# A one-layer S5 / RG-LRU trunk on one core: w_out's first sums one block sooner, one block split by VectorE, three columns at the head of gate's first half

## The chip, the cores and the metric

One core of a Trainium2 chip runs the whole program. The metric is the device time of one execution in microseconds (us), and the figure of a kernel is the median of its runs; smaller is better. The kernel before takes 932.66 us, the median of 3 runs (932.24 to 932.68).

## What is computed

The reference is one decoder layer over 1024 tokens and 1024 channels in float32. What matters here is its end:

```python
merged = jax.nn.sigmoid(gate_s) * z_s + jax.nn.sigmoid(gate_l) * z_l
x = x + rms_norm(merged @ w_out[i], g_post[i])
x = x + (p[i] @ w_ple[i]) * jax.nn.sigmoid(x @ w_ple_gate[i])
return x
```

So two products of 1024 x 1024 matrices follow each other (w_out, then w_ple_gate), and between them stands a normalisation over the channels, whose statistic needs all channels of a token.

## The kernel before

**Arithmetic.** Channels lie on the partitions, tokens on the free axis. Every float32 factor is split into two fp32r parts, hi (ScalarE's rounding copy) and lo (the rest), and `three` (L314 to L318) issues three matmuls of 128x128 by 128x512 for a block: hi by hi (L316), then hi of the weights by lo of the data and lo of the weights by hi of the data (L318). The product with w_out (like that with w_bl) is done by a recursion that needs fewer block products: seven products of quarters instead of eight, with sums of quarters of the weights (S1 to S4) and of the data (T1 to T4).

**Weights.** `weight_plan` writes the order of all weights down as a list of *quads* of four 128x128 blocks each, which TensorE takes one after the other. A "plain" quad is half of a chunk of eight blocks. The quads "O2", "S3", "S1", "S4" or "O4" belong to a pair of chunks and hold sums of them. The class `Weights` serves the list: `fetch` loads chunks on SP's queue into four raw tiles (`wraw`, 512 KB each), and a raw tile is loaded again only when all quads made from it are split; `sum` lets GpSimd add up the sums (tensor_tensor at L194, float32, both inputs in SBUF: S1 = A21 + A22, S2 = S1 - A11, S3 = A11 - A21, S4 = A12 - S2); `make` writes the hi part on ScalarE (L222) into a ring of six tiles (`wq`); the lo part comes in one of two ways. For plain quads of `BY_DMA` (w_bs, w_out, w_ple_gate, except for the last 16 quads) ScalarE writes the negative of the source (L225) and a DMA issued by GpSimd adds the source minus hi in the memory's path (L226, `accum_op=add`):

```python
if q[0] == "plain" and BLOCKS[q[1][0]][0] in self.BY_DMA and i < len(QUADS) - 2 * ND:
    nc.scalar.activation(lo, src, AF.Copy, scale=-1.0)
    nc.gpsimd.dma_start(lo.bitcast(F32), src, accum_op=ALU.add)
else:
    self.owed.append((i, lo, src, hi))
```

For all others VectorE subtracts (`lows`, L234). `ahead`, called before each product, makes quads up to four further than TensorE's place, splits one fewer, and starts sums up to two further than that. `sum` returns at an "O2" quad when the quad before it isn't made yet (L186).

**Order of the work.** TensorE, VectorE, ScalarE and GpSimd run their instructions in the order in which the program writes them (a manual schedule); pieces of background work (`bg`, generators) are advanced by `tick` after each product. The part around the change:

1. The product with w_out. Four products into banks oX (B11; quads 0 to 3 of w_out), two more into the first two oX banks (B21; quads 4 and 5; these are the last plain quads ahead of the sums), then four groups of oY, oZ, oW and oV with the sums S2, S3, S1 and S4. Meanwhile VectorE and ScalarE finish the data's parts: `t_raw` (L1385 to L1393) forms T2 and T3 of the last row, `t1_ops` T1. `op_split` takes hi on ScalarE (L1364) and lo on VectorE (L1371).
2. Six more products into oV, while `post_half(1)` normalises the tokens of half 1: it forms x1 (L1562, L1563) and its parts hi (L1364) and lo (L1371), eight rows one after the other.
3. `gate_half(1)`: columns of w_ple_gate by x1 of half 1. Its first two columns run over the rows 0 to 3 of x1 first (columns 0, 1), then over rows 4 to 7 (columns 0, 1), so that TensorE has work while the later rows are formed; then come columns 2 to 7 one by one. Beside it `post_half(0)` squares the last six rows of half 0 (ScalarE L1484, VectorE adds them to ssq, L1489) and TensorE sums them over the channels (`pst_post`, L388), ahead of column 4. `finish` (L1588 to L1592) takes a column out: sigmoid on ScalarE, which needs another activation table (ACT_TABLE_LOAD), a product and a sum on VectorE (L1590, L1591), and the store.
4. `gate_half(0)`: the eight columns by x1 of half 0.

In the prediction, "gate's quad 0, 1, ..." counts the quads of item 3 in TensorE's order; quad 4 is the first whose lo part is made after the last row of x1.

Of the kernel before, what the change touches and what calls it, by code (L numbers as in the profile page):

```python
# [20 lines left out]
ND = 8  # L21
# [15 lines left out]
def weight_plan():  # L37
    blocks, quads = [], []

    def chunk(names):  # L40
        first = len(blocks)
        blocks.extend(names)
        return (first, len(names))

    def cut(c):
        for o in range(0, c[1], 4):
            quads.append(("plain", c, o, min(4, c[1] - o)))

    def col(name, m, ks):
        return [(name, k, m) for k in ks]  # L50

    def plain(names):
        for o in range(0, len(names), 8):
            cut(chunk(names[o:o + 8]))

    for m in range(0, ND, 2):
        plain(col("w_ple", m, range(2)) + col("w_ple", m + 1, range(2)))
    lo, hi = range(4), range(4, ND)
    plain(col("w_in", 0, lo) + col("w_in", 1, lo))
    plain(col("w_in", 2, lo) + col("w_in", 0, hi))  # L60
    plain(col("w_in", 1, hi) + col("w_in", 2, hi))
    plain(col("w_in", 3, range(ND)))
    for m in (*range(36, 44), *range(28, 36), 4, 5):
        plain(col("w_in", m, range(ND)))

    def gated(m, head):
        c = chunk(col("w_in", m, range(ND)))
        quads.append(("plain", c, 0, 4))
        if head >= 0:
            plain([("w_a", head, 0), ("w_x", head, 0)])  # L70
        quads.append(("plain", c, 4, 4))

    for m in range(NL):
        gated(8 + m, m - 1)
        plain(col("w_in", 18 + m, range(ND)))
    gated(6, NL - 1)
    plain(col("w_in", 7, range(ND)))
    hi2 = range(8, NL)
    for ks in (lo, hi2, hi):
        if ks is hi2:  # L80
            plain([b for m in range(0, ND, 2) for b in col("w_bl", m, hi2)])
            continue
        for m in (0, 4):
            plain(col("w_bl", m, ks) + col("w_bl", m + 2, ks))
    for j in range(NS):
        plain(col("w_glu", 4 + j, range(NS)) + col("w_glu", j, range(NS)))
    for m in range(0, ND, 2):
        c0, c1 = (chunk(col("w_bl", m + i, range(8))) for i in range(2))
        for part in ("O2", "S1", "P", "S3", "S4", "A22"):
            if part == "P":  # L90
                plain(col("w_bl", m, hi2) + col("w_bl", m + 1, hi2))
            else:
                quads.append((part, c0, c1, 4))
    for n in range(0, ND, 2):
        plain([b for d in F_ROWS[n:n + 2] for b in col("w_bs", d, range(NS))])

    def outs(m, ks):
        cut(chunk(col("w_out", m, ks) + col("w_out", m + 2, ks)))

    for m, ks in ((0, lo), (4, lo), (0, hi)):  # L100
        outs(m, ks)
    for m in range(0, ND, 2):
        c0, c1 = (chunk(col("w_out", m + i, range(ND))) for i in range(2))
        quads.extend((part, c0, c1, 4) for part in ("O2", "S3", "S1", "O4" if m else "S4"))
    for m, ks in ((1, hi), (5, hi), (4, hi)):
        outs(m, ks)
    cs = [chunk(col("w_ple_gate", m, range(ND))) for m in range(ND)]
    for h in range(2):
        if not h:
            for ks in (lo, hi):  # L110
                cut(chunk(col("w_ple_gate", 0, ks) + col("w_ple_gate", 1, ks)))
        for c in cs[0 if h else 2:]:
            cut(c)
    return blocks, quads

# [15 lines left out]


LAST = chunk_users()


class Weights:
# [42 lines left out]
    def sum(self, upto):  # L179
        G = self.nc.gpsimd  # L180
        while len(self.ready) <= min(upto, len(QUADS) - 1):
            i = len(self.ready)
            self.fetch(i)
            q = QUADS[i]
            s = self.sums
            if q[0] == "O2" and len(self.done) < i:  # L186
                return

            def add(name, a, b, op, into=None):
                if into is None:  # L190
                    s[name] = self.tmp.tile([P, HT], F32, tag=name, name=f"w{name}_{i}")
                else:
                    s[name] = s[into]
                G.tensor_tensor(s[name], s[a], s[b], op)  # L194

            if q[0] == "plain":
                _, c, o, n = q
                self.ready.append((self.raws[c][:, o * P:(o + n) * P], n))
                continue
            if q[0] in FIRST:  # L200
                r0, r1 = (self.raws[c] for c in q[1:3])
                s.update(A11=r0[:, :HT], A12=r0[:, HT:], A21=r1[:, :HT], A22=r1[:, HT:])
            if q[0] == "O2":
                self.lows(i)
                add("S1", "A21", "A22", ALU.add)
                add("S2", "S1", "A11", ALU.subtract)
            if q[0] in ("S4", "O4"):
                add("S4", "A12", "S2", ALU.subtract, "S2")
            if q[0] == "S3":
                add("S3", "A11", "A21", ALU.subtract, "A21")  # L210
            self.ready.append((s[q[0].replace("O", "S")], 4))

    def make(self, upto):
        nc = self.nc
        while len(self.done) <= min(upto, len(QUADS) - 1):
            i = len(self.done)
            self.sum(i)
            src, n = self.ready[i]
            t = self.ring.tile([P, 2, 4, P], F32R, tag="q", name=f"wq{i}")
            hi = t[:, 0].rearrange("p b m -> p (b m)")[:, :n * P]  # L220
            lo = t[:, 1].rearrange("p b m -> p (b m)")[:, :n * P]
            nc.scalar.activation(hi, src, AF.Copy)  # L222
            q = QUADS[i]
            if q[0] == "plain" and BLOCKS[q[1][0]][0] in self.BY_DMA and i < len(QUADS) - 2 * ND:
                nc.scalar.activation(lo, src, AF.Copy, scale=-1.0)  # L225
                nc.gpsimd.dma_start(lo.bitcast(F32), src, accum_op=ALU.add)  # L226
            else:
                self.owed.append((i, lo, src, hi))
            self.done.append(t)
# [23 lines left out]
def tile_hybrid_trunk(  # L253
# [1315 lines left out]
    def gate_half(h, hl):  # L1569
        def rhs(k, _):  # L1570
            return hl(0, k), hl(1, k)

        first = {}
        if h:
            for n in range(4):
                q, m = n // 2, n % 2
                if not q:
                    first[m] = bank(f"ps_pg{h}{m}")
                W.ahead()
                for b, wb in enumerate(W.next()):  # L1580
                    three(first[m], wb, rhs(4 * q + b, h), q + b == 0, q * b == 3)
                tick()
        for m in range(ND):
            pl = plp[:, m % 4, :]
            nc.sync.dma_start(pl, ple_d[m][:, HALF[h]])
            sb = sbp[:, m % 4, :]

            def finish(ps, cs):  # L1588
                S.activation(sb[:, cs], ps, AF.Sigmoid)
                V.tensor_tensor(sb[:, cs], sb[:, cs], pl[:, cs], ALU.mult)  # L1590
                V.tensor_tensor(sb[:, cs], sb[:, cs], x1(m, h)[:, cs], ALU.add)  # L1591
                nc.sync.dma_start(out[m * P:(m + 1) * P, h * HT + cs.start:h * HT + cs.stop], sb[:, cs])  # L1592

            if h or m < ND - 1:
                finish(first.get(m) or plain(ND, rhs, f"pg{h}{m}", (h,))[h], slice(0, HT))
                continue
            W.ahead()
            wq = [W.next(), W.next()]
            for c in range(2):
                ps = bank(f"ps_pgz{c}")[:, :HT // 2]  # L1600
                cs = slice(c * HT // 2, (c + 1) * HT // 2)
                for k in range(ND):
                    three(ps, wq[k // 4][k % 4], [v[:, cs] for v in rhs(k, h)], k == 0, k == ND - 1)
                if c == 0:
                    finish(ps, cs)
                    continue
                cut = [slice(HT // 2, HT // 2 + P), slice(HT // 2 + P, HT)]
                for i, q in enumerate(cut):
                    S.activation(sb[:, q], ps[:, i * P:(i + 1) * P], AF.Sigmoid)
                for q in cut:  # L1610
                    V.tensor_tensor(sb[:, q], sb[:, q], pl[:, q], ALU.mult)
                    V.tensor_tensor(sb[:, q], sb[:, q], x1(m, h)[:, q], ALU.add)
                nc.sync.dma_start(out[m * P:(m + 1) * P, h * HT + cs.start:h * HT + cs.stop], sb[:, cs])
# [81 lines left out]
```

## Time and profile before

| | |
|---|---|
| median of 3 runs | 932.66 us (932.24 to 932.68) |
| the profiled execution | 932.37 us |
| its span, first to last instruction | 930.6 us |
| TensorE busy | 923.1 us, 99% of the span |
| VectorE, ScalarE, GpSimd busy | 625.0, 469.6, 150.3 us |
| mean granted TensorE clock | 0.999 of full speed |
| the chain that ended last | 96% TensorE, 2% VectorE |

The span is counted from the first to the last instruction on the core; the time of the execution has some 1.8 us around it. The page gives busy time by engine, the trace gives single instructions: start, duration, engine, line, what is written and read, and in brackets how long the engine had been idle before and which instruction released it. TensorE's durations are modelled: matmuls overlap, so a step of three matmuls takes less than the sum of its rows, and the distance from one start to the next is what counts.

### The profile page before, as it was taken

The page shows a single profiled execution, that of the slowest core. Times are in us where ns is not written, and L with a number is a line of the kernel's source. Part 1 is how long each engine was busy: PE and PEld are TensorE (multiplying, and loading weights), DVE is VectorE, ACT ScalarE, POOL GpSimd, SP SyncE. Part 2 cuts the span into 40 slices and gives each one's busy share as a digit, 9 for nine tenths or more (in the row PEclk, how much of TensorE's full clock was granted, in tenths as well). Part 3 has the DMA queues.
Part 4 walks back from the last instruction along what each step waited for, and adds up shares of the span by engine and source line. Part 5 has one row for each costly group of instructions (what it writes and reads, how often), then busy time and mean ns, then how long its engine had stood idle before and what let it go on. Part 6 is the DMA issues. An engine that isn't in the chain of part 4 may idle for free.

```text
span 930.6 us, 11716 instructions
## 1 busy us (share of the span) xinstructions
PE 923.1 (99%) x4228; PEld 759.7 (82%) x4228; DVE 625.0 (67%) x977; ACT 469.6 (50%) x714; POOL 150.3 (16%) x159
## 2 busy tenths in 40 slices
PE   9999999999999999999999999999999999999997
PEld 7888888888888888888888888888888887887876
DVE  6985566666664446776666667687862798886863
ACT  6643233444443257666666668444434355558531
POOL 1318012212220000000000000022322126422100
PEclk9999999999999999999999999999999999999999
DMA  9745456554623211111111117811479965499951
GB/s 356 277 126 158 126 141 168 173 166 138 178 90 107 74 29 52 51 51 45 52 51 51 52 44 208 296 41 57 141 261 238 271 164 203 122 244 231 301 181 52
DMA packets 70442, 134.21 MB, mean 144 GB/s; under 512 B 18416, under 2 KB 32880, under 8 KB 70384
## 3 DMA queue, kind: packets, MB, share of 16 engines
q1 hardware_dynamic: 64768, 122.72, 41.5%
q0 software_dynamic: 5472, 10.49, 6.5%
q8 instruction: 33, 0.54, 0.2%
q10 hardware_dynamic: 144, 0.26, 0.1%
q14 instruction: 25, 0.20, 0.1%
HBM read 95.30 MB, written 27.53 MB: 132 GB/s over the span
## 4 chain that ended last, share of the span: by engine, by line
PE 96%; DVE 2%; issue 0%; DMA 0%; ACT 0%
PE ps_L L318 16%; PE ps_L L316 8%; PE ps_rg L318 8%; PE ps_rx L318 8%; PE ps_pg L318 6%; PE ps_rx L316 4%; PE ps_rg L316 4%; PE ps_F L318 3%; PE ps_u L318 3%; PE bZ L318 3%; PE ps_pg L316 3%; PE pg L318 2%; PE bW L318 2%; PE bX L318 2%; PE ps_ple L318 2%; PE ps_ea L318 2%
## 5 line engine op out<-in xcount | busy, mean ns | idle before, releaser
L318 PE MATMUL ps_L<-hB,wq 128*128 128x512 f32 x640 | 197.4, 390 | 0.0
L318 PEld LDWEIGHTS ps_L<-hB,wq 128*128 128x128 f32 x640 | 120.2, 188 | 24.5
L316 PE MATMUL ps_L<-hB,wq 128*128 128x512 f32 x320 | 127.0, 397 | 0.0
L222 ACT ACTIVATE wq<-wraw 128x512 fp32r<-128x512 f32 (+1 forms) x188 | 112.5, 614 | 24.3 <-issue 9.4
L234 DVE TENSOR_TENSOR wq<-wraw,wq 128x512 fp32r<-128x512 f32 (+1 forms) x152 | 104.0, 700 | 3.2 <-ACT wq L222 3.2
L318 PE MATMUL ps_rg<-hB,wq 128*128 128x512 f32 x320 | 98.7, 390 | 0.0
L318 PE MATMUL ps_rx<-hB,wq 128*128 128x512 f32 x320 | 98.7, 390 | 0.0
L318 PE MATMUL ps_pg<-x1hl,wq 128*128 128x512 f32 x240 | 75.2, 394 | 0.5 <-DVE x1hl L1371 0.5
L316 PEld LDWEIGHTS ps_L<-hB,wq 128*128 128x128 f32 x320 | 60.1, 188 | 13.4 <-issue 1.7
L318 PEld LDWEIGHTS ps_rg<-hB,wq 128*128 128x128 f32 x320 | 60.1, 188 | 12.9
L318 PEld LDWEIGHTS ps_rx<-hB,wq 128*128 128x128 f32 x320 | 60.1, 188 | 12.9
L1075 DVE SCALAR_TENSOR_TENSOR c<-ps_rx,cp_t,c 128x1023 f32<-128x1023 f32 (+2 forms) x30 | 38.5, 1282 | 47.6 <-ACT c L1073 46.9
L194 POOL TENSOR_TENSOR wS<-wraw 128x512 f32<-128x512 f32 x8 | 11.9, 1486 | 356.8 <-DMA wraw<-w_blocks 349.4
L316 PE MATMUL ps_rx<-hB,wq 128*128 128x512 f32 x160 | 62.5, 391 | 0.0
L316 PE MATMUL ps_rg<-hB,wq 128*128 128x512 f32 x160 | 62.5, 391 | 0.0
L318 PEld LDWEIGHTS ps_pg<-x1hl,wq 128*128 128x128 f32 x240 | 44.7, 188 | 11.8 <-DVE x1hl L1371 1.8
L1012 ACT ACTIVATE sg<-ps_L 128x1024 f32<-128x1024 f32 x20 | 20.5, 1026 | 59.6 <-issue 52.5
L226 POOL DMA_DIRECT2D wq<-wraw x36 | 31.8, 883 | 100.7 <-ACT wq L225 68.7
L316 PE MATMUL ps_pg<-x1hl,wq 128*128 128x512 f32 x120 | 47.1, 393 | 0.0
L318 PE MATMUL ps_u<-hB,wq 128*128 128x512 f32 x128 | 39.7, 392 | 0.4 <-DVE hB L733 0.4
L318 PE MATMUL ps_F<-ys,wq 128*128 128x512 f32 x128 | 39.4, 389 | 0.0
L1083 ACT ACT_TABLE_LOAD x9 | 11.5, 1283 | 51.2 <-DVE yr L1112 51.2
(360 smaller groups left out, 1930.4 us busy)
## 6 DMA issues: line engine op xcount, KB each, us to landing
wraw<-w_blocks SPq DMA_DIRECT2D x95, 512.0 KB
wq<-wraw POOLq DMA_DIRECT2D x36, 256.0 KB, 5.5
xt<-x_t SPq DMA_DIRECT2D x8, 512.0 KB
ple_d<-ple_sb SPq DMA_DIRECT2D x8, 512.0 KB
wn<-sbt SPq DMA_DIRECT2D x8, 512.0 KB
sgl_d<-sg SPq DMA_DIRECT2D x8, 512.0 KB
wn<-pt_d SPq DMA_DIRECT2D x16, 256.0 KB
sgs_d<-sg SPq DMA_DIRECT2D x8, 512.0 KB
```

What stands on the lines that cost most here:

```text
L194: G.tensor_tensor(s[name], s[a], s[b], op)
L222: nc.scalar.activation(hi, src, AF.Copy)
L226: nc.gpsimd.dma_start(lo.bitcast(F32), src, accum_op=ALU.add)
L234: self.nc.vector.tensor_tensor(lo, src, hi.bitcast(F32), ALU.subtract)
L316: T.matmul(ps, wh, xh, start=start, stop=False, skip_group_check=more)
L318: T.matmul(ps, a, b, start=False, stop=stop and a is (wh if xl_last else wl), skip_group_check=more)
L1012: S.activation(t, ps, AF.Sigmoid)
L1075: V.scalar_tensor_tensor(c[:, d:], ps[:, :NT - d], w_[3 - d], c[:, d:], ALU.mult, ALU.add)
L1083: S.activation(sq, ps, AF.Sigmoid)
```

## The change

Three edits. `AHEAD` lets `sum` begin the first "O2" of w_out (quad number `FIRST_OUT`) when the quad before the one before it is made, that is one block sooner. `BY_V` names that one block ahead (quad `FIRST_OUT - 1`, the last plain quad before the sums): its lo part is made by VectorE's subtraction, no longer by ScalarE's negative copy and the adding DMA. And gate's first half runs its first rows over three columns (0, 1, 2) and then the last rows over the same three; `weight_plan` puts the quads in that order.

```diff
--- before.py
+++ after.py
@@ -107,9 +107,10 @@
     cs = [chunk(col("w_ple_gate", m, range(ND))) for m in range(ND)]
     for h in range(2):
         if not h:
-            for ks in (lo, hi):
+            for i, ks in enumerate((lo, hi)):
                 cut(chunk(col("w_ple_gate", 0, ks) + col("w_ple_gate", 1, ks)))
-        for c in cs[0 if h else 2:]:
+                quads.append(("plain", cs[2], 4 * i, 4))
+        for c in cs[0 if h else 3:]:
             cut(c)
     return blocks, quads
 
@@ -131,6 +132,9 @@
 
 
 LAST = chunk_users()
+FIRST_OUT = max(i for i, q in enumerate(QUADS) if q[0] == "O2") - 12
+BY_V = (FIRST_OUT - 1,)
+AHEAD = {i: i == FIRST_OUT for i, q in enumerate(QUADS) if q[0] == "O2"}
 
 
 class Weights:
@@ -183,7 +187,7 @@
             self.fetch(i)
             q = QUADS[i]
             s = self.sums
-            if q[0] == "O2" and len(self.done) < i:
+            if q[0] == "O2" and len(self.done) < i - AHEAD[i]:
                 return
 
             def add(name, a, b, op, into=None):
@@ -221,7 +225,7 @@
             lo = t[:, 1].rearrange("p b m -> p (b m)")[:, :n * P]
             nc.scalar.activation(hi, src, AF.Copy)
             q = QUADS[i]
-            if q[0] == "plain" and BLOCKS[q[1][0]][0] in self.BY_DMA and i < len(QUADS) - 2 * ND:
+            if q[0] == "plain" and BLOCKS[q[1][0]][0] in self.BY_DMA and i < len(QUADS) - 2 * ND and i not in BY_V:
                 nc.scalar.activation(lo, src, AF.Copy, scale=-1.0)
                 nc.gpsimd.dma_start(lo.bitcast(F32), src, accum_op=ALU.add)
             else:
@@ -1572,8 +1576,8 @@
 
         first = {}
         if h:
-            for n in range(4):
-                q, m = n // 2, n % 2
+            for n in range(6):
+                q, m = n // 3, n % 3
                 if not q:
                     first[m] = bank(f"ps_pg{h}{m}")
                 W.ahead()
```

What it does to the order on the engines, first where w_out's sums begin. GpSimd's instructions there before (a DMA row is the adding DMA of one quad, `wS` are the sums S1 and S2, wq_5908 is the block ahead of them):

```order
L226 DMA wq_5834<-wraw_5515 128x512
L226 DMA wq_5882<-wraw_5586 128x512
L226 DMA wq_5908<-wraw_5586 128x512
L194 TENSOR_TENSOR wS_158_5916<-wraw_5754 128x512
L194 TENSOR_TENSOR wS_158_5918<-wS_158_5916,wraw_5752 128x512
```

and with the change (the same block is now wq_5912):

```order
L230 DMA wq_5834<-wraw_5515 128x512
L230 DMA wq_5882<-wraw_5586 128x512
L198 TENSOR_TENSOR wS_158_5886<-wraw_5754 128x512
L198 TENSOR_TENSOR wS_158_5888<-wS_158_5886,wraw_5752 128x512
L198 TENSOR_TENSOR wraw_5754<-wraw_5752,wraw_5754 128x512
```

The DMA of the block ahead is gone from GpSimd's queue, and the three sums that need nothing else (S1, S2, and S3, which is written over a raw tile) stand right behind the DMA of the block before it.

VectorE at the same place, before (mT are the data's parts T2, T3 and T1; wq_5940 is the first summed quad):

```order
L1388 TENSOR_TENSOR mtmp<-mg_5538,mg_5536 128x512
L1390 TENSOR_TENSOR mg_5536<-mg_5538,mg_5536 128x512
L1371 TENSOR_TENSOR mT_5540<-mtmp,mT_5539 128x512
L1392 TENSOR_TENSOR mg_5538<-mg_5538,mtmp 128x512
L1371 TENSOR_TENSOR mT_5542<-mg_5536,mT_5541 128x512
L1371 TENSOR_TENSOR mT_5935<-mg_5535,mT_5934 128x512 x2
L1371 TENSOR_TENSOR mT_5935<-mg_5536,mT_5934 128x512
L234 TENSOR_TENSOR wq_5940<-wS_158_5918,wq_5940 128x512
```

and with the change:

```order
L1392 TENSOR_TENSOR mtmp<-mg_5538,mg_5536 128x512
L1394 TENSOR_TENSOR mg_5536<-mg_5538,mg_5536 128x512
L1375 TENSOR_TENSOR mT_5540<-mtmp,mT_5539 128x512
L1396 TENSOR_TENSOR mg_5538<-mg_5538,mtmp 128x512
L1375 TENSOR_TENSOR mT_5542<-mg_5536,mT_5541 128x512
L1375 TENSOR_TENSOR mT_5929<-mg_5535,mT_5928 128x512 x2
L238 TENSOR_TENSOR wq_5912<-wraw_5586,wq_5912 128x512
L1375 TENSOR_TENSOR mT_5929<-mg_5536,mT_5928 128x512
L238 TENSOR_TENSOR wq_5934<-wS_158_5888,wq_5934 128x512
```

VectorE has one instruction more, the lo part of the block ahead (wq_5912), behind the seven instructions of T2, T3 and T1.

ScalarE where the last rows of x1 are formed for gate's first half, before (wq_6557 is gate's quad 4):

```order
L1364 ACTIVATE x1hl_6442<-x_6368 128x512 x2
L1364 ACTIVATE x1hl_6442<-x_6369 128x512 x2
L222 ACTIVATE wq_6557<-wraw_6351 128x512
L225 ACTIVATE wq_6557<-wraw_6351 128x512
L1484 ACTIVATE sq<-mix_5999 128x512
L222 ACTIVATE wq_6575<-wraw_6351 128x512
```

and with the change (wq_6554 is gate's quad 4 now, rows 4 to 7 of column 1 instead of rows 0 to 3 of column 2):

```order
L1368 ACTIVATE x1hl_6441<-x_6367 128x512 x2
L1368 ACTIVATE x1hl_6441<-x_6368 128x512 x2
L226 ACTIVATE wq_6554<-wraw_6350 128x512
L229 ACTIVATE wq_6554<-wraw_6350 128x512
L1488 ACTIVATE sq<-mix_5998 128x512
L226 ACTIVATE wq_6574<-wraw_6300 128x512
```

Quad 4 keeps its place behind the last two pairs of x1's rows; only the blocks that it holds are others.

VectorE behind that, before (`ssq` is the sum of squares that `pst_post` reads, `sbp` a gate column on its way out):

```order
L1371 TENSOR_TENSOR x1hl_6444<-x_6369,x1hl_6442 128x512 x2
L1489 TENSOR_TENSOR ssq<-ssq,sq 128x512 x3
L1590 TENSOR_TENSOR sbp<-sbp,plp 128x512
L1591 TENSOR_TENSOR sbp<-sbp,x_6366 128x512
L1590 TENSOR_TENSOR sbp<-sbp,plp 128x512
L1591 TENSOR_TENSOR sbp<-sbp,x_6366 128x512
L1489 TENSOR_TENSOR ssq<-ssq,sq 128x512 x2
L1590 TENSOR_TENSOR sbp<-sbp,plp 128x512
L1591 TENSOR_TENSOR sbp<-sbp,x_6367 128x512
L1489 TENSOR_TENSOR ssq<-ssq,sq 128x512
L392 TENSOR_SCALAR diags<-pst_post_6724 128x4
```

and with the change:

```order
L1375 TENSOR_TENSOR x1hl_6443<-x_6368,x1hl_6441 128x512 x2
L1493 TENSOR_TENSOR ssq<-ssq,sq 128x512 x5
L1594 TENSOR_TENSOR sbp<-sbp,plp 128x512
L1595 TENSOR_TENSOR sbp<-sbp,x_6365 128x512
L1594 TENSOR_TENSOR sbp<-sbp,plp 128x512
L1595 TENSOR_TENSOR sbp<-sbp,x_6365 128x512
L1594 TENSOR_TENSOR sbp<-sbp,plp 128x512
L1595 TENSOR_TENSOR sbp<-sbp,x_6366 128x512
L1493 TENSOR_TENSOR ssq<-ssq,sq 128x512
```

The last addition to ssq stands behind three columns' pairs of instructions in both, but all six of these now come after five additions, where two pairs had come after three and one after two more. On ScalarE the table load and the sigmoids of the first columns accordingly stand behind the ring tiles of gate's quads 4 to 9 and all six squares, where they had stood behind quads 4 to 7 and four squares.

On SP's queue a load of x ahead of gate moves behind two weight loads, and the first stores of gate's columns move behind one more weight load.

## Rows read from the trace of the kernel before

**Rows 1.** The page: span; busy us (share) xinstructions by engine

```profile
span 930.6 us, 11716 instructions
...
PE 923.1 (99%) x4228; PEld 759.7 (82%) x4228; DVE 625.0 (67%) x977; ACT 469.6 (50%) x714; POOL 150.3 (16%) x159
```

**Rows 2.** Waits of TensorE over the span: us in total, times, longest

```profile
PE ps_pg L318 <- DVE x1hl L1371: 0.5, 1, 0.5
...
PEld ps_pg L318 <- DMA wq<-wraw: 0.4, 1, 0.4
```

**Rows 3.** Timeline, PE, 766 to 773: start, us, what [idle before <-releaser]

```profile
768.79 0.39 PE L316 MATMUL oX<-mB,wq 128*128 128x512 f32 x1
...
771.51 0.40 PE L316 MATMUL oY<-mT,wq 128*128 128x512 f32 x1
...
772.43 0.50 PE L318 MATMUL oY<-mT,wq 128*128 128x512 f32 x1 [0.30 <-DVE wq L234]
...
772.78 0.39 PE L316 MATMUL oY<-mT,wq 128*128 128x512 f32 x1
```

**Rows 4.** Timeline, DVE, 760 to 782

```profile
761.71 0.69 DVE L1388 TENSOR_TENSOR mtmp<-mg,mg 128x512 f32<-128x512 f32 x1
...
765.75 3.70 DVE L1371 TENSOR_TENSOR mT<-mg,mT 128x512 fp32r<-128x512 f32 x2 [0.75 <-ACT mT L1364]
...
771.09 0.69 DVE L1371 TENSOR_TENSOR mT<-mg,mT 128x512 fp32r<-128x512 f32 x1 [1.64 <-ACT mT L1364]
...
771.70 0.69 DVE L234 TENSOR_TENSOR wq<-wS,wq 128x512 fp32r<-128x512 f32 x1
...
778.12 3.48 DVE L1371 TENSOR_TENSOR mB<-mg,mB 128x512 fp32r<-128x512 f32 x2
```

**Rows 5.** Timeline, POOL, 760 to 782

```profile
761.14 0.86 POOL L226 DMA_DIRECT2D wq<-wraw  x1 [6.32 <-ACT wq L225]
...
765.57 1.62 POOL L194 TENSOR_TENSOR wS<-wraw 128x512 f32<-128x512 f32 x1
```

**Rows 6.** Window: us; busy PE PEld DVE ACT POOL; clock, DMA share, GB/s

```profile
758.00:760.00 2.00, 2.00 (x11) 1.65 (x10) 1.93 (x4) 0.82 (x2) 0.00 (x0) 1.00 0.02 3
```

**Rows 7.** Timeline, PE, 839 to 848

```profile
841.09 0.39 PE L316 MATMUL ps_pg<-x1hl,wq 128*128 128x512 f32 x1
...
843.31 0.39 PE L316 MATMUL ps_pg<-x1hl,wq 128*128 128x512 f32 x1
...
846.03 0.39 PE L316 MATMUL ps_pg<-x1hl,wq 128*128 128x512 f32 x1
...
847.00 0.39 PE L316 MATMUL ps_pg<-x1hl,wq 128*128 128x512 f32 x1
```

**Rows 8.** Timeline, ACT, 841 to 851

```profile
841.87 0.61 ACT L222 ACTIVATE wq<-wraw 128x512 fp32r<-128x512 f32 x1
...
847.60 0.62 ACT L1484 ACTIVATE sq<-mix 128x512 f32<-128x512 f32 x1
...
848.23 1.28 ACT L1589 ACT_TABLE_LOAD   x1
```

**Rows 9.** Timeline, POOL, 841 to 851

```profile
843.30 0.86 POOL L226 DMA_DIRECT2D wq<-wraw  x1 [8.28 <-ACT wq L225]
```

**Rows 10.** DMA issues, 843 to 844: KB each, us to landing

```profile
wq<-wraw POOLq DMA_DIRECT2D x1, 256.0 KB, 3.3
```

**Rows 11.** Timeline, SP's queue, 836 to 862

```profile
839.00 15.20 SPq L163 DMA_DIRECT2D wraw<-w_blocks  x3
```

**Rows 12.** Timeline, DVE, 843 to 862

```profile
850.16 0.69 DVE L1590 TENSOR_TENSOR sbp<-sbp,plp 128x512 f32<-128x512 f32 x1 [2.78 <-ACT sbp L1589]
...
851.49 0.69 DVE L1590 TENSOR_TENSOR sbp<-sbp,plp 128x512 f32<-128x512 f32 x1
...
856.09 0.69 DVE L1489 TENSOR_TENSOR ssq<-ssq,sq 128x512 f32<-128x512 f32 x1
```

**Rows 13.** Chain that ended last, 850 to 860: start, us, what

```profile
857.40 0.79 PE pst_post L388 x8
```

## The prediction

> **What bounds the kernel now.** I read the page first: TensorE is busy 923.1 of 930.6 us [rows 1], so only what makes it wait, or fills less of its time, can move the end. So next the waits of TensorE and of its weight loads. Two entries lie where the change works: a wait of matmuls for VectorE's x1hl, and a weight load that waits for the adding DMA of a quad [rows 2]; a third, of oY for VectorE's wq, stands in the timeline [rows 3]. The listed idle times understate the loss, since a row of a matmul is longer than its share of the pace. The pace is read from two starts that are one product (four steps) apart: 771.51 - 768.79 = 2.72 us, so 0.68 a step [rows 3]. Then each loss is the distance of starts less the pace:
> - oY: 772.78 - 771.51 - 0.68 = 0.59 us [rows 3].
> - gate, rows 6 and 7 of x1: 843.31 - 841.09 - 2 x 0.68 = 0.86 us [rows 7].
> - gate, quad 4: 847.00 - 846.03 - 0.68 = 0.29 us [rows 7], the wait for the adding DMA.
>
> Together 1.74 us, 0.19% of the time: even if all of it went, the result would be inside what a measurement of this kernel can tell from no change, about 0.2% or 1.87 us. Last I read the timelines of VectorE, GpSimd and ScalarE there, to see what the waits hang on.
>
> **Edit 1, sums sooner and the block ahead split by VectorE.** Removed: one negative copy on ScalarE and one DMA issue on GpSimd, neither of which TensorE waits for. Added: one subtraction on VectorE, 0.60 us by the distance of two of its starts (771.70 after 771.09, 0.61) [rows 4]. Moved: GpSimd's sums. Before, they begin at 765.57 [rows 5]; now they can begin right behind the DMA of the block before, issued at 761.14 [rows 5], at some 761.7. Their inputs don't hold them: the DMA engines are idle at 758 to 760 (share 0.02) [rows 6], so loads issued by then have landed.
>
> That the oY wait goes seems safe: the summed quad's hi waits for GpSimd today, and the sums come some 4 us sooner. I count -0.59.
>
> What is late next is the block ahead. Its lo part is used third in the first step of the second B21 product, which starts at 768.79 [rows 3]. On VectorE it stands behind five instructions of T2 and T3 from 761.71 on and two of T1 from 765.75 on [rows 4]. Undisturbed, the two of T1 would take 2 x 0.60 and the new one end at 766.95 + 0.69 = 767.64, in time. But VectorE isn't undisturbed beside GpSimd's sums: the two of T1 take 3.70 us today, and another pair 3.48 at 778.12 [rows 4]. Each of these waits out one GpSimd sum: (3.70 - 1.20) / 2 = 1.25 us more apiece. Today three such blocks hit work that nobody waits for soon; with the change all three sums that need nothing else fall between 761.7 and 767, ahead of the new instruction. Three blocks are 3.75 us; VectorE's idle time before T1 (0.75 [rows 4], and 0.20 within the five, which take 765.75 - 0.75 - 761.71 = 3.29 us against 5 x 0.60 + 0.09) absorbs 0.95. So the lo part ends at 767.64 + 3.75 - 0.95 = 770.44. In the oY case the next step began 0.39 us after VectorE's end (771.70 + 0.69 to 772.78) [rows 3, 4], so here at 770.83, where it would be 768.79 + 0.68 = 769.47: +1.36 us. Bounds: 0 if GpSimd is the one to be blocked; 770.44 + 0.95 + 0.39 - 769.47 = 2.31 us if none of the idle time absorbs. I take 1.36, since ScalarE, which sets that idle time, has one copy less there.
>
> Here a rule bears on the choice. The Trainium skill, "SBUF — State Buffer", section "Who interferes with whom", says that a VectorE instruction with two SBUF inputs and a GpSimd instruction that reads SBUF share a port as an exclusive lock, and that issue order decides who blocks. The trace agrees that VectorE blocks (3.70 us for two); the rule alone would also allow a VectorE queue without gaps to keep the port, which makes the term 0 instead of 1.36. That is a rival below.
>
> **Edit 2, three columns.** Rows 4 to 7 of x1 are now needed 2.72 us later, so the 0.86 us at rows 6 and 7 go. But quad 4 is late next. Its copies on ScalarE start at 841.87, behind the last row of x1 [rows 8]; its DMA is issued at 843.30 [rows 9] and takes 3.3 us [rows 10], so it lands at 846.6, and TensorE goes on to the next step at 847.00 [rows 7]. None of this is moved by the edit: quad 4 has the same place on ScalarE. TensorE arrives 0.86 us sooner and waits 0.86 longer. Net 0. The bounds are -0.86 (the DMA lands that much sooner) and 0; the row is 3.3 us without a queue ahead of it, so I take 0.
>
> Then half 0's statistic. `pst_post` starts at 857.40 today [rows 13], after the last addition to ssq, which starts at 856.09 [rows 12] and ends at 856.78. Now that addition stands behind three pairs for finished columns, and these behind the table load, and that behind six squares. ScalarE: from the copy at 841.87 to the fourth square at 847.60 are 11 instructions, 0.52 apiece [rows 8]; the sixth square is six further, at 850.72, and ends at 851.34. The table load follows at once, as today (847.60 + 0.62, then 848.23) [rows 8]. The first product of a finished column starts 850.16 - 848.23 = 1.93 us after the table load [rows 8, 12], now at 853.28. A pair takes 851.49 - 850.16 = 1.33 [rows 12], so the last addition starts at 853.28 + 3 x 1.33 = 857.27 and ends at 857.96. TensorE, back in step since quad 4, stands ready at 857.40 and waits 0.04 more (as oY did, 772.43 after 772.39) [rows 3, 4]: +0.60 us. Bounds: 0 (if the squares run sooner) and +1.3 (one more pair's time).
>
> SP's queue: the raw tile of column 2 now stays in use until quad 5 is split, so the load issued at 839.00 [rows 11] waits for quad 5's DMA, which lands three ScalarE instructions after quad 4's, at 846.6 + 3 x 0.52 = 848.2, some 9 us later. ScalarE needs that load behind the table load and three sigmoids (851.34 + 1.28 + 3 x 0.52, near 854), so 6 us remain for it; I count 0. The x load that moves belongs to rows formed after all of this product, and the stores are awaited by nobody: 0.
>
> **Sum.** -0.59 + 1.36 - 0.86 + 0.86 + 0.60 = +1.37 us. The profiled execution took 932.37 us, its span 930.6; so 933.74, and by the median of the runs, which lies 0.29 above it, 934.03. I say 933.9: a little slower, not by what can be told.
>
> **Rivals.**
> 1. *VectorE keeps the port*; GpSimd is blocked instead and the new lo part is in time. -0.59 + 0 + 0.60 = 0.0, 932.7. For it: VectorE's queue has few gaps there. Against: the pairs of 3.70 and 3.48. 15%.
> 2. *The statistic isn't late*, because squares or sigmoids run sooner than counted: +0.77, 933.4. Against it: the order on VectorE is fixed. 12%.
> 3. *The change does only what it says*: both waits go and nothing comes in their place, the DMA's wait at quad 4 staying at 0.29: -1.45, 931.2. It needs the block ahead in time, quad 4's DMA sooner and the squares sooner, all three. 5%.
> 4. *Slower*: ScalarE slides along with VectorE. Its copy for the third T3 part waits for a VectorE instruction that is itself blocked, and the copies for T1 stand behind it, so VectorE's idle time isn't absorbed but moved. The term at the second B21 product is then 2.31: -0.59 + 2.31 + 0.60 = +2.32, 935.0. It decides from the point where T1's copies end later than VectorE's own work ahead of them (some 768.5). For it: today VectorE waits 0.75 for just these copies [rows 4]. Against: ScalarE has one copy less ahead of them. 13%.
>
> That the change doesn't do what it says at all is excluded by the orders printed above.
>
> **How the numbers follow.** The forecast (933.3 to 934.6) has 55%; the rivals 15, 12, 5 and 13. The range 932.2 to 934.9 holds the forecast, rivals 1 and 2 with the runs' spread, and the lower edge of rival 4; it leaves out rival 3 and most of rival 4. The bound of 0.2% lies at 930.8 and 934.5: rival 3 is inside it, so faster has only 2%; slower has rival 4 and the top of the forecast, 15%; the rest is 83%.
>
> **What would show it.** In the profile after: no wait of oY; a wait of the second B21 product (oX) for VectorE's wq of about 1 us; VectorE's instructions of T2 and T3 at 1.6 to 1.9 us apiece instead of 0.69; no wait for x1hl in gate, but one for the adding DMA of about 1 us; `pst_post` waiting for ssq by 0.6 us. I am wrong if the oX product starts its second step within 0.7 us of its first, or if `pst_post` follows the matmuls before it without a gap.

## The result, and the profile after

The changed kernel takes 934.06 us, the median of 14 runs (933.58 to 935.12), against 932.49 for the kernel before on the same chips (14 runs, 932.13 to 932.75): 1.57 us more, a ratio of 1.0018 with a 95% interval of 1.001 to 1.0026. Forecast were 933.9 and a chance of 83% for a change within 0.2%. The interval lies above 1, so the change makes the kernel slower, by 0.18%; what the profile shows is whether it did so for the reasons given.

The page of the profile after, the lines that answer to [rows 1]:

```profile
span 932.9 us, 11713 instructions
...
PE 922.2 (99%) x4228; PEld 758.2 (81%) x4228; DVE 627.1 (67%) x978; ACT 468.9 (50%) x713; POOL 148.6 (16%) x158
```

The profiled execution took 934.69 us, 0.63 above the median of its kernel. 0.62 of its 2.32 us over the profiled execution before are already there when the second B21 product starts (769.41 against 768.79 [rows 3]); 0.60 of it at the first matmul of ps_u (34.15 against 33.55), long ahead of the change, so distances and not clock times are compared below.

The waits of TensorE (us in total, times, longest), of the changed kernel, answering to [rows 2]:

```profile
PE ps_pg L322 <- DMA wq<-wraw: 1.5, 2, 0.9
...
PE oX L322 <- DVE wq L238: 0.9, 1, 0.9
```

The wait for VectorE's x1hl is gone from the list, and so is oY's. In their places stand a wait of oX for VectorE's wq and two waits for the adding DMA. TensorE's timeline at the start of the sums (start, duration, engine, line and operation, idle before and releaser) answers to [rows 3]:

```profile
769.41 0.39 PE L320 MATMUL oX<-mB,wq 128*128 128x512 f32 x1
...
770.92 0.50 PE L322 MATMUL oX<-mB,wq 128*128 128x512 f32 x1 [0.90 <-DVE wq L238]
771.26 0.39 PE L320 MATMUL oX<-mB,wq 128*128 128x512 f32 x1
...
773.32 0.40 PE L320 MATMUL oY<-mT,wq 128*128 128x512 f32 x1
...
774.03 0.39 PE L320 MATMUL oY<-mT,wq 128*128 128x512 f32 x1
```

The second B21 product loses 771.26 - 769.41 - 0.68 = 1.17 us in its first step; oY's first step takes 774.03 - 773.32 = 0.71 and loses nothing that can be told. VectorE's timeline there, to be read beside [rows 4]:

```profile
762.28 2.18 DVE L1392 TENSOR_TENSOR mtmp<-mg,mg 128x512 f32<-128x512 f32 x1
764.38 1.77 DVE L1394 TENSOR_TENSOR mg<-mg,mg 128x512 f32<-128x512 f32 x1
766.08 1.78 DVE L1375 TENSOR_TENSOR mT<-mtmp,mT 128x512 fp32r<-128x512 f32 x1
...
770.19 0.68 DVE L238 TENSOR_TENSOR wq<-wraw,wq 128x512 fp32r<-128x512 f32 x1
```

and GpSimd's, beside [rows 5]:

```profile
761.72 0.86 POOL L230 DMA_DIRECT2D wq<-wraw  x1 [6.32 <-ACT wq L229]
762.28 1.61 POOL L198 TENSOR_TENSOR wS<-wraw 128x512 f32<-128x512 f32 x1
```

The sums now start right behind the DMA of the block before, as intended. The three instructions of VectorE that meet them take 2.18, 1.77 and 1.78 us, where the first took 0.69 before (the prediction had 1.6 to 1.9 for all five of T2 and T3; the other two meet no sum and take some 0.7). VectorE has no idle time between 762.28 and the lo part of the block ahead. The lo part of the block ahead starts at 770.19; TensorE goes on at 770.92.

Gate, TensorE's steps, answering to [rows 7] (the first two are the steps on row 6 and row 7 of x1 in the fourth product, which is the first over the rows 4 to 7):

```profile
845.03 0.39 PE L320 MATMUL ps_pg<-x1hl,wq 128*128 128x512 f32 x1
...
845.71 0.39 PE L320 MATMUL ps_pg<-x1hl,wq 128*128 128x512 f32 x1
...
846.39 0.39 PE L320 MATMUL ps_pg<-x1hl,wq 128*128 128x512 f32 x1
...
848.23 0.39 PE L320 MATMUL ps_pg<-x1hl,wq 128*128 128x512 f32 x1
...
855.79 0.39 PE L320 MATMUL ps_pg<-x1hl,wq 128*128 128x512 f32 x1
...
857.38 0.39 PE L320 MATMUL ps_pg<-x1hl,wq 128*128 128x512 f32 x1
```

Rows 6 and 7 and the first step of quad 4 behind them now follow each other at the pace of 0.68. Quad 4 loses 848.23 - 846.39 - 0.68 = 1.16, where it lost 0.29, and quad 7, which lost nothing before, loses 857.38 - 855.79 - 0.68 = 0.91. The DMAs of these two quads on GpSimd's queue, beside [rows 9]:

```profile
844.52 0.86 POOL L230 DMA_DIRECT2D wq<-wraw  x1 [8.28 <-ACT wq L229]
...
849.20 0.86 POOL L230 DMA_DIRECT2D wq<-wraw  x1 [0.70 <-ACT wq L229]
```

From issue to landing the first took 3.3 us, as before; the second, by the view of DMA issues (KB, us to landing),

```profile
wq<-wraw POOLq DMA_DIRECT2D x1, 256.0 KB, 7.8
```

took 7.8, where the DMA of the same quad took 5.8 before:

```profile
wq<-wraw POOLq DMA_DIRECT2D x1, 256.0 KB, 5.8
```

Beside it run two weight loads that SP's queue could issue only now, since the raw tiles of the first three columns had been in use until quads 4 and 5 were split. The first is issued at 847.97, where quad 4's DMA has just landed (844.52 + 3.3 = 847.82), the second at 849.51, where quad 5's has (846.08 + 3.4 = 849.48). The first of four, beside the one of [rows 11]:

```profile
847.97 12.06 SPq L167 DMA_DIRECT2D wraw<-w_blocks  x4
```

Added up: -0.59 + 1.17 - 0.86 + 0.87 + 0.91 = +1.50 us of the 1.57. `pst_post` does not wait.

### The profile page after: what moved, and what is told of

Same layout as the page of the kernel before. It is cut to its first block, busy times and chain, and to the rows that moved or that the text cites. A ratio compares the mean times of both kernels' runs of the same rounds, so it can differ in the third digit from the quotient of the medians.

```text
span 932.9 us, 11713 instructions
## 1 busy us (share of the span) xinstructions
PE 922.2 (99%) x4228; PEld 758.2 (81%) x4228; DVE 627.1 (67%) x978; ACT 468.9 (50%) x713; POOL 148.6 (16%) x158
## 4 chain that ended last, share of the span: by engine, by line
PE 89%; issue 4%; DVE 3%; DMA 2%; POOL 1%; ACT 0%; POOLq 0%; DVEq 0%
PE ps_L L322 16%; PE ps_L L320 8%; PE ps_rx L322 8%; PE ps_rg L322 8%; PE ps_pg L322 5%; PE ps_rg L320 4%; PE ps_rx L320 4%; PE ps_u L322 3%; PE bZ L322 3%; PE ps_F L322 3%; PE ps_pg L320 2%; PE pg L322 2%; PE bW L322 2%; PE bX L322 2%; PE ps_ea L322 2%
```

## The experiments

Ten kernels ran. Each was timed beside the kernel before on its chip, 11 runs; a ratio stands with its 95% interval. Distances of steps are read as above, start to start less 0.68.

**1. Edit 1 alone.** The plan and the loop of gate as before:

```diff
-            for n in range(6):
-                q, m = n // 3, n % 3
+            for n in range(4):
+                q, m = n // 2, n % 2
```

> Edit 1 alone (sums one block sooner, the block ahead split by VectorE), gate's columns as before. Theory (the two edits each put a new wait in the place of the old one, and add up): oY's 0.59 us goes, the second B21 product waits about 1.2 us for VectorE's lo part, gate keeps its 0.86 and 0.29: +0.6 us, about 933.1. Rival (edit 1 is worth its 0.59 and all the loss is gate's): -0.6 us, about 931.9, and no wait of oX.

Measured: 933.21 against 932.54, 1.0009 (1.0 to 1.0018), +0.67 us. oX waits for VectorE, oY doesn't; gate loses 0.87 and 0.30 as before. In the profiled execution, the longest of its 11, the second B21 product lost 1.75, more than in the changed kernel's, and the first one 0.39 in waiting for its own DMA. So the size varies between executions; what it varies with stands at the end of the next section.

**2. Edit 2 alone.** `AHEAD` all false, `BY_V = ()`:

> Edit 2 alone (three columns at the head of gate's first half), w_out's sums as before. Theory: the 0.86 us at x1's rows 6 and 7 goes and comes back at quad 4, whose step waits about 1.15 us for its adding DMA instead of 0.29; behind that about 0.9 us more, at gate's quad 7 (its DMA lands late) or at pst_post (ssq late): +0.9 us, about 933.4; oY still waits 0.59. Rival (edit 2 gains and edit 1 loses all of it): -0.6 to -0.9 us.

Measured: 933.44, 1.0012 (1.0003 to 1.0021), +0.90 us. The two parts add up to 0.67 + 0.90 = 1.57, what both together cost (that it agrees to the last digit is chance, since each part's interval is some 0.8 us to either side). Here quad 4 loses 1.15, quads 6 and 7 lose 0.16 and 0.34, and `pst_post` is late too. TensorE around it:

```profile
857.16 0.39 PE L320 MATMUL ps_pg<-x1hl,wq 128*128 128x512 f32 x1
...
858.14 1.02 PE L392 MATMUL pst_post<-ones,ssq 128*128 128x1 f32 x8
859.03 0.48 PE L320 MATMUL ps_pg<-x1hl,wq 128*128 128x512 f32 x1
```

and the last addition to ssq on VectorE:

```profile
857.31 0.68 DVE L1493 TENSOR_TENSOR ssq<-ssq,sq 128x512 f32<-128x512 f32 x1
```

That addition was forecast for 857.27 and starts at 857.31; `pst_post` follows its end by 0.15 us. From the step before to the step behind `pst_post` are 859.03 - 857.16 = 1.87 us, against 1.49 in the kernel before.

**3. The block ahead split by VectorE, the sums not begun sooner in the program** (gate as before):

```diff
-AHEAD = {i: i == FIRST_OUT for i, q in enumerate(QUADS) if q[0] == "O2"}
+AHEAD = {i: 0 for i, q in enumerate(QUADS) if q[0] == "O2"}
```

GpSimd's order stays that of edit 1, because without the block's DMA nothing stands between the sums and the DMA before them. What differs is VectorE's order.

> Only the block ahead split by VectorE, without beginning the sums a block sooner in the program, gate as before. GpSimd's order is the same as with edit 1 (its sums still follow the DMA of the block before), but on VectorE the lo part of the block ahead stands before the two instructions of T1 and not behind them. Theory (the wait of oX is VectorE's queue, stretched by GpSimd's port use): the lo part ends some 1.2 us sooner, oX waits at most 0.2, oY not at all: -0.4 to -0.6 us, about 932.0. Rival (a split by VectorE beside GpSimd's sums is late wherever it stands): oX still waits about 1 us, 933.1.

Measured: 931.97, 0.9997 (0.9988 to 1.0005), -0.57 us. Neither oX nor oY waits. On VectorE the sums stretch the same instructions as much as in edit 1, but the lo part (second row) starts at 768.95, where it started at 770.19 in the changed kernel:

```profile
762.24 2.18 DVE L1391 TENSOR_TENSOR mtmp<-mg,mg 128x512 f32<-128x512 f32 x1
...
768.95 0.68 DVE L237 TENSOR_TENSOR wq<-wraw,wq 128x512 fp32r<-128x512 f32 x1
```

So the wait of oX came from the lo part's place behind T1's instructions in a queue stretched by the sums; the one without the other is harmless. In the profiled execution, the longest of its 11 (933.33), TensorE also waits 0.96 us for an adding DMA at 871.50, in gate's second half, which this edit doesn't touch.

**4. Edit 1 without GpSimd's sums in that group** (the four sums are left out, and quarters of the weights stand in their place):

```diff
+            if FIRST_OUT <= i < FIRST_OUT + 4:
+                if q[0] == "O2":
+                    self.lows(i)
+                    s.update(S1=s["A21"], S2=s["A22"], S3=s["A11"], S4=s["A12"])
+                self.ready.append((s[q[0].replace("O", "S")], 4))
+                continue
```

> Edit 1 alone, with GpSimd's four sums of the first group of w_out left out (quarters of the weights stand in for them), so that GpSimd is idle while VectorE forms T2, T3, T1 and the lo part. Theory (the port): VectorE's instructions there take 0.69 us each and not 1.7 to 2.2, the lo part is done before its product begins, neither oX nor oY waits: about 932.0. Rival (VectorE's queue is too long by itself, or it waits for ScalarE): its instructions are as long as in edit 1's run or it idles, and oX still waits about 1 us, 933.1.

Measured: 931.87, 0.9994 (0.9985 to 1.0003), -0.67 us, and no wait of oX or oY. VectorE's first instructions of T2 and T3, and the lo part of the block ahead:

```profile
761.75 0.69 DVE L1397 TENSOR_TENSOR mtmp<-mg,mg 128x512 f32<-128x512 f32 x1
762.36 0.69 DVE L1399 TENSOR_TENSOR mg<-mg,mg 128x512 f32<-128x512 f32 x1
...
766.49 0.69 DVE L243 TENSOR_TENSOR wq<-wraw,wq 128x512 fp32r<-128x512 f32 x1
```

With GpSimd idle each takes 0.69 us and the lo part starts at 766.49, in the same order on VectorE as in edit 1. The stretch is GpSimd's doing. The Trainium skill, "SBUF — State Buffer", section "Who interferes with whom", says that a VectorE instruction with two SBUF inputs contends with a GpSimd instruction that reads SBUF, and that their shared ports are an exclusive lock. These runs agree (2.18 us beside a sum and 0.69 without one for the same instruction).

**5. The sums begun sooner, the block ahead by its DMA** (`BY_V = ()`, gate as before):

> Only the sums begun one block sooner; the block ahead keeps its adding DMA, gate as before. GpSimd now adds S1 and S2 before it issues that DMA, and ScalarE's negative copy, which the DMA needs, comes later because VectorE, stretched by the sums, holds up the copies ahead of it. Theory (port and queue order): the DMA is issued near 768 and lands 3 to 5 us later, oX waits 2 us or more, oY not: +1.4 us or more, 934 or above, so the split by VectorE is what keeps edit 1's own loss small. Rival (the DMA is soon enough and VectorE's split is the whole loss): 931.9, no wait of oX.

Measured: 933.62 against 932.50, 1.0015 (1.0006 to 1.0024), +1.12 us. The DMA of the block ahead now stands behind two sums on GpSimd's queue,

```profile
767.57 0.86 POOL L229 DMA_DIRECT2D wq<-wraw  x1 [2.55 <-ACT wq L228]
```

takes 3.3 us to land, and TensorE waits for it in the second B21 product:

```profile
770.92 0.50 PE L321 MATMUL oX<-mB,wq 128*128 128x512 f32 x1 [1.53 <-DMA wq<-wraw]
```

The step loses 1.80 us. The mechanism is the one expected; the time is a miss (934 or above was forecast, and a wait of 2 us or more), as the DMA landed at the lower of the two durations allowed for. So beginning the sums sooner is what makes the loss. That the split by VectorE makes it smaller fits the step (1.17 in the changed kernel, 1.80 here) and the medians (+0.67 with edit 1, +1.12 here), but the intervals of the two runs overlap.

**6. Edit 2 alone, column 2 first in the second pass:**

```diff
-                q, m = n // 3, n % 3
+                q, m = n // 3, (0, 1, 2, 2, 0, 1)[n]
```

(and the plan's quads in that order.)

> Edit 2 alone, but in its second pass column 2 comes first (then 0, 1), so that the raw tile of column 2 is free two quads sooner and the next weights' load is issued at some 840 and not at 848. Theory (the time behind gate's quad 4 is set by the last addition to ssq, three pairs of VectorE behind the table load; the late DMAs at quads 6 and 7 lie in its shadow): those DMA waits go, pst_post waits the more, the time stays that of edit 2 alone, 933.4 (933.2 to 933.6). Rival (the late DMAs set it): about 0.5 us less, 932.9.

Measured: 933.52, 1.0011 (1.0002 to 1.002), the time of edit 2 alone. The next weights are issued at 841.42 and no DMA behind quad 4 is waited for; in their place TensorE waits for ssq:

```profile
857.11 0.39 PE L323 MATMUL ps_pg<-x1hl,wq 128*128 128x512 f32 x1
...
858.70 1.02 PE L395 MATMUL pst_post<-ones,ssq 128*128 128x1 f32 x8 [0.74 <-DVE ssq L1496]
859.58 0.48 PE L323 MATMUL ps_pg<-x1hl,wq 128*128 128x512 f32 x1
```

From step to step 2.47 us, 0.98 more than the 1.49 of the kernel before: the late DMAs at quads 6 and 7 did lie in the statistic's shadow. GpSimd issues its DMAs here at the same distance of 1.56 us as in the changed kernel, with one load on SP's queue (848.88) between the two at 841.42 and 854.69, and the DMAs of quads 6 and 7 take 3.4 and 6.0 us where they took 5.7 and 7.8. So it is the loads beside them, and not GpSimd's own queue, that makes them late.

**7. Edit 2 alone, gate's quad 4 split by VectorE:**

```diff
+GATE = len(QUADS) - 4 * ND
-BY_V = ()
+BY_V = (GATE + 4,)
```

> Edit 2 alone, with gate's quad 4 split by VectorE and not by the adding DMA. Theory (two bounds in a row: quad 4's DMA, and behind it ssq): quad 4's 1.15 us goes, but TensorE then waits for ssq, which comes only one ScalarE copy, 0.52 us, sooner: 932.9 (932.7 to 933.2), with the waits moved to pst_post and the quads just ahead of it. Rival (quad 4's DMA alone gives the gain back): all of 1.15 is won, 932.3 or less.

Measured: 933.92, 1.0013 (1.0004 to 1.0022): a miss in the time. The 11 runs fall apart, five from 932.78 to 933.31 and six from 933.92 to 934.45. The profiled execution took 933.95, and its waits are

```profile
PE ps_ple L321 <- ACT wq L227: 2.1, 2, 1.3
PE pst_post L393 <- DVE ssq L1494: 1.1, 1, 1.1
...
PE oY L323 <- DVE wq L239: 0.7, 1, 0.7
```

quad 4's wait is gone and `pst_post` waits for ssq instead, as expected; but 2.1 us are listed in the first products of the program, after which the first matmul of ps_u starts at 34.15 (33.64 in the run of edit 2), and oY loses 0.96 instead of 0.56. Neither place is touched by this edit. From the first step of quad 4 to the first behind `pst_post` there are 16 steps. With edit 2 alone the first of these two rows is

```profile
845.22 0.39 PE L320 MATMUL ps_pg<-x1hl,wq 128*128 128x512 f32 x1
```

and the second the one at 859.03 above: 859.03 - 845.22 - 16 x 0.68 = 2.93 us lost, the time of `pst_post` included. With quad 4 split by VectorE they are

```profile
846.15 0.39 PE L321 MATMUL ps_pg<-x1hl,wq 128*128 128x512 f32 x1
...
859.45 0.48 PE L321 MATMUL ps_pg<-x1hl,wq 128*128 128x512 f32 x1
```

so 2.42: 0.51 less, near the 0.52 of one copy. The start (0.51 later) and oY (0.40 more) outweigh that in this execution, and the median time does not show it; the kept profile is of the slower six.

**8. Quads 4 and 5 by VectorE** (`BY_V = (GATE + 4, GATE + 5)`), run because of that miss:

> Edit 2 alone, with gate's quads 4 and 5 split by VectorE (between the run with quad 4 alone and the one with quads 4 to 7). Theory (ScalarE's copies ahead of the last square set the end of this stretch): each copy fewer brings the last addition to ssq 0.52 us forward; against edit 2 alone 1.04 us less, 932.4 (932.0 to 932.7). Rival (the number of copies does not matter and the run with quad 4 alone was no gain): 933.4 or more.

Measured: 932.28, 0.9997 (0.9989 to 1.0006), 1.16 us below edit 2 alone. From quad 4 to behind `pst_post` the steps lose 858.32 - 845.55 - 10.88 = 1.89 us:

```profile
845.55 0.39 PE L321 MATMUL ps_pg<-x1hl,wq 128*128 128x512 f32 x1
...
858.32 0.48 PE L321 MATMUL ps_pg<-x1hl,wq 128*128 128x512 f32 x1
```

**9. Quads 4 to 7 by VectorE** (`BY_V = tuple(range(GATE + 4, GATE + 8))`):

> Edit 2 alone, with gate's quads 4 to 7 split by VectorE. Theory: quad 4's wait goes, and four ScalarE copies fewer bring the last addition to ssq 2.1 us forward, so that pst_post waits 0.2 us at most; against edit 2 alone some 1.9 us less: 931.5 (931.2 to 931.9). Rival (VectorE's four subtractions, each ahead of an addition to ssq, take the place of the copies): 932.5 or more, with VectorE busy without gaps from 844 on.

Measured: 931.43 against 932.49, 0.9991 (0.9982 to 0.9999), 2.01 us below edit 2 alone. No wait is left in gate. VectorE's subtraction for quad 4, the addition behind it and the last addition:

```profile
843.41 0.68 DVE L239 TENSOR_TENSOR wq<-wraw,wq 128x512 fp32r<-128x512 f32 x1
844.01 0.68 DVE L1494 TENSOR_TENSOR ssq<-ssq,sq 128x512 f32<-128x512 f32 x1
...
855.98 0.69 DVE L1494 TENSOR_TENSOR ssq<-ssq,sq 128x512 f32<-128x512 f32 x1
```

The steps from quad 4 to behind `pst_post` lose 857.70 - 845.97 - 10.88 = 0.85 us here, what `pst_post` itself takes (0.81 in the kernel before):

```profile
845.97 0.39 PE L321 MATMUL ps_pg<-x1hl,wq 128*128 128x512 f32 x1
...
857.70 0.49 PE L321 MATMUL ps_pg<-x1hl,wq 128*128 128x512 f32 x1
```

So with no, one, two and four copies fewer the loss is 2.93, 2.42, 1.89 and 0.85: 0.5 a copy, the distance of two of ScalarE's starts (0.52 [rows 8]). ScalarE's copies ahead of the last square set the end of this stretch.

**10. What the runs point to:** block ahead by VectorE as in experiment 3, three columns as in 6, quads 4 to 7 as in 9:

```diff
+BY_V = (FIRST_OUT - 1, *range(GATE + 4, GATE + 8))
+AHEAD = {i: 0 for i, q in enumerate(QUADS) if q[0] == "O2"}
```

> Both waits of the kernel before attacked without the new ones: the block ahead split by VectorE but not begun sooner in the program, three columns with column 2 first in the second pass, and gate's quads 4 to 7 split by VectorE. Theory (the terms add): 0.6 us from oY and some 1.1 us from gate, 930.9 (930.6 to 931.3). Rival (something that these waits hid, a late DMA or the clock, comes out): no faster than the better of its parts, 931.5 or more.

Measured: 930.69 (930.47 to 931.63), 0.998 (0.9971 to 0.9989): 1.80 us less than the kernel before and 3.4 less than the changed one. All waits of TensorE that its profile lists lie in the start of the program:

```profile
PE warm L505 <- DVE halfpi L299: 1.1, 1, 1.1
PE ps_ple L324 <- ACT wq L230: 0.6, 1, 0.6
PE ps_u L326 <- DVE hB L741: 0.4, 1, 0.4
```


## Why the prediction was right

| term | forecast | measured in the changed kernel |
|---|---|---|
| oY's wait goes | -0.59 | -0.59 (left: 0.03) |
| oX waits for the lo part | +1.36 | +1.17 |
| x1's rows 6 and 7 | -0.86 | -0.86 |
| quad 4 waits for its DMA | +0.86 | +0.87 |
| the statistic (`pst_post` waits for ssq) | +0.60 | 0 |
| SP's queue (the loads moved behind quads 4 and 5) | 0 | +0.91, as a wait of quad 7 for its DMA |
| sum | +1.37 | +1.50 |

**Edit 1.** The step that decided was the choice of 1.36 between 0 and 2.31 for the second B21 product. Three blocked instructions were costed at 1.25 us each, 3.75; they cost 1.49 + 1.08 + 1.09 = 3.66 over 0.69 each, and the idle time ahead of T1 absorbed part of it, as assumed: none of it is left in VectorE's queue. Experiment 4 shows the cause by taking the sums away, experiment 3 by moving only the lo part. Rival 1, VectorE keeping the port, is excluded by the three long rows; rival 4, none of the idle time absorbed, would have been 2.31. In edit 1's own profiled execution the product lost 1.75, between 1.36 and 2.31; the median of its runs (+0.67, where -0.59 + 1.36 is +0.77) fits 1.36.

**Edit 2.** That the gain at x1's rows would come back at quad 4 to the last tenth held: its DMA hangs on ScalarE's place behind the last row of x1, which the edit doesn't move. Experiments 7 to 9 take that DMA away.

**The statistic** is where the prediction failed, though the sum held. It named as a sign of being wrong that `pst_post` follows the matmuls before it without a gap, and so it does: it starts at 859.45, a pace of 0.69 behind the last step of quad 7 (858.76), without waiting. The step that failed is "SP's queue ... I count 0". The loads held back by the raw tiles (the first until quad 4's DMA has landed, not quad 5's, as the prediction had it) are not awaited themselves, but they run beside the adding DMAs, and quad 7's lands late (7.8 us). That wait of 0.91 covers the statistic: the last addition to ssq, below, ends at 859.15, some 0.15 us before it would have to be waited for.

```profile
858.76 0.39 PE L320 MATMUL ps_pg<-x1hl,wq 128*128 128x512 f32 x1
...
859.45 0.95 PE L392 MATMUL pst_post<-ones,ssq 128*128 128x1 f32 x8
```

```profile
858.47 0.68 DVE L1493 TENSOR_TENSOR ssq<-ssq,sq 128x512 f32<-128x512 f32 x1
```

The way to that addition was forecast well: TensorE reaches gate 1.22 us later than before (845.03 - 841.09 - 2.72), so it stands at 857.25 by the clock of the kernel before, against 857.27. Without the late DMAs (experiment 6) it is waited for and the time is the same, so the term stands behind the other, but at 0.98 and not 0.60. Of this difference 0.16 has a reason: 857.40 [rows 13] was taken as the start of `pst_post`, but it is the chain's first piece; in TensorE's own timeline of the kernel before the first of the eight matmuls starts at 857.24.

```profile
857.24 0.95 PE L388 MATMUL pst_post<-ones,ssq 128*128 128x1 f32 x8
```

The two errors, 0.19 too much for oX and 0.31 too little behind quad 4, nearly cancel. That the sum came so close is luck: a wait that was counted as nothing stands in the place of the one that was forecast, and is not far from it in size. Rival 2 (a statistic in time, because squares or sigmoids run sooner) is excluded by the addition's start and by the wait of `pst_post` in experiment 6, rival 3 (nothing new) by experiment 2, where edit 2 alone costs 0.90.

How much oX and oY lose varies between executions (oY 0.55 to 1.31 in the six profiles with w_out's sums as before), and it varies with VectorE's lag behind TensorE. Where oY loses 0.55 to 0.59, it starts 9.80 to 9.82 us behind VectorE's first instruction of T2's last row; in experiment 7 that is 9.41 (0.96 lost), in experiment 9 it is 9.06 (1.31 lost). The lag goes with waits of VectorE for the load of `msr` 20 to 34 us earlier: 0.44 us in experiment 7, 0.81 in experiment 9, 0.84 and 0.20 in experiment 1's longer wait of oX; none of the other profiles has one. What stays open is why that load comes late in some executions.

## What to carry to other kernels

Where one engine is busy 99% of the time, take a wait out only together with the next event that the same product needs: read when that lands, and compare it with where the engine will stand without the wait (quad 4's DMA gave back 0.87 of 0.86). Work that is moved ahead on GpSimd lands on VectorE's instructions of that time, so the instruction that somebody waits for belongs ahead of those that nobody waits for in VectorE's queue (experiment 3: 1.2 us from its place in the order). And a queue that gets shorter on ScalarE by a copy that VectorE can take over in its gaps was worth the copy's full 0.5 us each, where a statistic hung on the end of that queue.

## What the hardware showed that was not expected

- GpSimd and VectorE took turns one for one here: VectorE's queue had no gap when the sums came, and still each of three sums got in, each blocking one VectorE instruction (2.18, 1.77, 1.78 us), while the sums themselves took 1.61 to 1.74 us (1.29 for the one at 783.31 in the same profile).
- The adding DMA of 256 KB, 3.3 us from issue to landing for quad 4, took 7.8 us for quad 7, beside two loads on SP's queue, and 6.0 in experiment 6, beside one.
- The waits of the first products for ScalarE's first weights differ between executions of unchanged code (0.6 us in the kernel before, 2.1 in experiment 7's), and the first matmul of ps_u starts anywhere from 33.30 to 34.16 in the twelve profiles, more than half of what the change itself is worth: such a difference in one execution's span says nothing until the steps behind the start are compared.
